# The same instructions of a two-layer hybrid decoder trunk, ordered on each engine by a timeline model of time

## The chip, the cores and the metric

One core of a Trainium2 chip. The time is that of the whole program on the device, in microseconds (us); the runs shown are single executions, and their median is the kernel's time. A profile is one more execution, recorded by the hardware profiler, and its span goes from the first to the last instruction.

## What is computed

A sequence of 256 tokens of width 1024 goes through two layers, everything in fp32. Cut to what matters:

```python
for i in range(DEPTH):                      # DEPTH = 2
    h = h + 0.5 * swiglu(rmsnorm(h), ...)   # first feed-forward half step
    u = rmsnorm(h)
    (q, c_kv, q_idx, w_idx, k_idx, x_pool, z, xbc, dt_raw, gate_raw) = split(u @ w_in[i])
    y_attn = dsa_attention(...)             # indexer picks 64 keys, 8 heads
    y_pool = pool_mixer(x_pool, ...)        # windows of 2, 4, 8, 16
    y_ssd  = ssd_mixer(z, xbc, dt_raw, ...) # causal conv, chunked scan, gate, norm
    merged = (g_attn * (y_attn @ w_br_attn[i]) + g_pool * (y_pool @ w_br_pool[i])
              + g_ssd * (y_ssd @ w_br_ssd[i]))
    h = h + merged @ w_out[i]
    h = h + 0.5 * swiglu(rmsnorm(h), ...)   # second half step
    h = h + sigmoid(rmsnorm(h) @ w_g[i]) * (p[i] @ w_p[i])   # per-layer embedding
return rmsnorm(h)
```

## The kernel before

The weights are streamed once, in units of 128 x 1024 fp32 (512 KB). `load` (L128 to L130) does three things for each unit: SP fetches it as `raw`, ACT casts it to a high part `whi` (L129), and DVE takes the residue `wlo` = `raw` - `whi` (L130). A product is then three matmuls, L152 (high by high), L153 (low activation by high weight) and L154 (high activation by low weight, the one that needs `wlo`), each of 128 x 128 weights by 256 columns; a unit gives 24 of them. There are four buffers each of `raw`, `whi` and `wlo`, and `unit` asks for a unit three ahead of its use. PSUM is used as four banks for the large products (tag "mm") and four for everything else ("aux"), both from `bank`.

Each layer goes through these stages:

- FFN1 (about 15 to 200 us in layer 1), then the norm before the mix. `rnorm` sums squares (L203, L206 on ACT, L208 on DVE), adds over partitions with a matmul by ones (L232), takes the reciprocal root on DVE (L181 to L195), makes two diagonal matrices (L239, L240) and spreads the factor over the partitions with two matmuls (L246), which ACT copies to `rs_r` (L248).
- The mix, 200 to 430 us: input projections, a first weave of columns, conv (L618, L620, L623), indexer (L656 to L679) and gates; then a second weave, in which the generators of the scan (`ssd`, L834 to L875), attention (L640, L701 to L726), the pools and the gates take turns (`weave`, L609). L712 are transposes; L845 is the scan's matmul into 64 columns, L640 the attention's matmul from 64 rows.
- The lift: eight steps of 48 matmuls. A step fills one bank p1 (attention and pools, 24 matmuls) and half a bank p2 (scan, 24 matmuls). L587 reads p1 and frees it; L592 reads p2 and frees it, but L591 before it multiplies by `rs_r`, the factor of the scan's norm, so that no p2 is freed before that `rs_r` is there. L593 and L594 add up, L168 and L169 split the result for the output product (L312 and on).
- FFN2 and the per-layer embedding, then the second layer alike, and a final norm.

What sets the order: each engine runs its own list in order. The program is written in one sequence, and the tile scheduler makes the engines' lists from it, by the instructions' dependences, buffers and priorities; the kernel steers it with the order of its generators and with `issue_after`. Line 1113 in `program`, which builds everything twice (the second time with the order of the weight units that the first has noted), opens the context that does this.

In the rows and orders below, a name like `wlo_3022` is one buffer's content, numbered in the order of the program; the profile leaves these numbers out.

Of the kernel before, what the change touches and what calls it, by code (L numbers as in the profile page):

```python
# [1103 lines left out]
def program(arrays):  # L1104

    order = None
    for last in (False, True):
        nc = bacc.Bacc("TRN2", target_bir_lowering=False, num_devices=1,
                       dynamic_dma_scratch_size=1024)
        ins = {k: nc.dram_tensor(f"in_{k}_dram", v.shape, F, kind="ExternalInput").ap()  # L1110
               for k, v in arrays.items()}
        out = nc.dram_tensor("out_0_dram", (2, P, D), F, kind="ExternalOutput").ap()
        with tile.TileContext(nc) as tc, ExitStack() as ctx:
            b = Builder(ctx, tc, ins, out, order)
            b.build()
        order = b.used
    return nc
# [8 lines left out]
```

## Time and profile before

| | us |
|---|---|
| median of 3 runs (lowest to highest) | 1342.96 (1341.96 to 1343.63) |
| the profiled execution's own time | 1343.21 |
| its span | 1341.4 |
| busy in the span: PE | 1319.0 (98%) |
| busy: DVE | 1047.8 (78%) |
| busy: ACT | 744.4 (55%) |
| granted TensorE clock, mean | 0.998 |

The program has 28355 instructions. Busy time of PE is the union of its matmuls as the profile draws them; their ends are modelled. Weight fetches move 248 MB in the span, a mean of 185 GB/s.

### The profile page before, as it was taken

The page shows a single profiled execution, that of the slowest core. Times are in us where ns is not written, and L with a number is a line of the kernel's source. Part 1 is how long each engine was busy: PE and PEld are TensorE (multiplying, and loading weights), DVE is VectorE, ACT ScalarE, POOL GpSimd, SP SyncE. Part 2 cuts the span into 40 slices and gives each one's busy share as a digit, 9 for nine tenths or more (in the row PEclk, how much of TensorE's full clock was granted, in tenths as well). Part 3 has the DMA queues.
Part 4 walks back from the last instruction along what each step waited for, and adds up shares of the span by engine and source line. Part 5 has one row for each costly group of instructions (what it writes and reads, how often), then busy time and mean ns, then how long its engine had stood idle before and what let it go on. Part 6 is the DMA issues. An engine that isn't in the chain of part 4 may idle for free.

```text
span 1341.4 us, 28355 instructions
## 1 busy us (share of the span) xinstructions
PE 1319.0 (98%) x11502; PEld 1299.4 (97%) x11502; DVE 1047.8 (78%) x1967; ACT 744.4 (55%) x1209; POOL 3.4 (0%) x17
## 2 busy tenths in 40 slices
PE   8999999999999999999999999999999999999997
PEld 7999999999899999999999999999998999999997
DVE  7777668987989787766887776789789887777666
ACT  5554446557754555544654554556577545555454
POOL 0000000000000000000000000000000000000000
PEclk9999999999999999999999999999999999999999
DMA  7666656566456666666656666646654666666661
GB/s 257 191 194 197 192 160 197 158 196 187 146 178 188 193 203 190 193 198 192 188 180 199 191 195 193 186 148 189 203 165 135 198 196 197 197 190 197 193 193 62
DMA packets 72386, 248.25 MB, mean 185 GB/s; under 512 B 7936, under 2 KB 10304, under 8 KB 72256
## 3 DMA queue, kind: packets, MB, share of 16 engines
q1 hardware_dynamic: 71392, 245.17, 59.3%
q8 instruction: 90, 1.47, 0.5%
q10 hardware_dynamic: 864, 1.28, 0.3%
q14 instruction: 40, 0.33, 0.1%
HBM read 245.33 MB, written 1.08 MB: 184 GB/s over the span
## 4 chain that ended last, share of the span: by engine, by line
PE 88%; DVE 8%; ACT 2%; issue 1%; DMA 0%; SPq 0%; DVEq 0%; ACTq 0%
PE mm L152 27%; PE mm L153 27%; PE mm L154 27%; DVE wlo L130 3%; ACT whi L129 1%; PE aux L640 1%; DVE t L620 1%; PE aux L726 1%; PE aux L845 1%; PE aux L152 1%; PE aux L153 1%; PE aux L154 1%; DVE rs_t L193 0%; DMA raw<-in_w_dram 0%; PE aux L712 0%
## 5 line engine op out<-in xcount | busy, mean ns | idle before, releaser
L129 ACT CAST whi<-raw 128x1024 fp32r<-128x1024 f32 (+1 forms) x457 | 475.8, 1045 | 484.9 <-issue 245.1
L152 PE MATMUL mm<-uh,whi 128*128 128x256 f32 x2560 | 712.9, 279 | 7.4 <-ACT whi L146 6.3
L154 PE MATMUL mm<-uh,wlo 128*128 128x256 f32 x2560 | 710.4, 278 | 2.8 <-DVE wlo L130 2.6
L153 PE MATMUL mm<-ul,whi 128*128 128x256 f32 x2560 | 711.5, 278 | 0.1
L130 DVE TENSOR_TENSOR wlo<-raw,whi 128x1024 fp32r<-128x1024 f32 (+1 forms) x457 | 554.2, 1215 | 200.8 <-ACT whi L129 198.1
L152 PEld LDWEIGHTS mm<-uh,whi 128*128 128x128 f32 x2560 | 482.0, 188 | 10.5 <-ACT whi L146 6.3
L154 PEld LDWEIGHTS mm<-uh,wlo 128*128 128x128 f32 x2560 | 482.2, 188 | 4.8 <-DVE wlo L130 3.7
L153 PEld LDWEIGHTS mm<-ul,whi 128*128 128x128 f32 x2560 | 482.2, 188 | 3.0 <-issue 2.1
L154 PE MATMUL mm<-gh,wlo 128*128 128x256 f32 x704 | 194.3, 276 | 0.0
L152 PE MATMUL mm<-gh,whi 128*128 128x256 f32 x704 | 194.3, 276 | 0.0
L153 PE MATMUL mm<-gl,whi 128*128 128x256 f32 x704 | 194.3, 276 | 0.0
L154 PEld LDWEIGHTS mm<-gh,wlo 128*128 128x128 f32 x704 | 132.1, 188 | 0.0
L153 PEld LDWEIGHTS mm<-gl,whi 128*128 128x128 f32 x704 | 132.1, 188 | 0.0
L152 PEld LDWEIGHTS mm<-gh,whi 128*128 128x128 f32 x704 | 132.1, 188 | 0.0
L152 PE MATMUL mm<-a,whi 128*128 128x256 f32 x256 | 70.9, 277 | 0.0
L153 PE MATMUL mm<-a,whi 128*128 128x256 f32 x256 | 70.7, 276 | 0.0
L154 PE MATMUL mm<-a,wlo 128*128 128x256 f32 x256 | 70.7, 276 | 0.0
L152 PEld LDWEIGHTS mm<-a,whi 128*128 128x128 f32 x256 | 48.1, 188 | 0.0
L153 PEld LDWEIGHTS mm<-a,whi 128*128 128x128 f32 x256 | 48.1, 188 | 0.0
L154 PEld LDWEIGHTS mm<-a,wlo 128*128 128x128 f32 x256 | 48.1, 188 | 0.0
L345 DVE TENSOR_TENSOR t<-mm,rs_r 128x256 f32<-128x256 f32 x88 | 37.3, 423 | 10.1
L172 ACT ACTIVATE uh<-h,cc 128x256 fp32r<-128x256 f32 x64 | 31.8, 504 | 18.5 <-DVE h L317 13.7
(213 smaller groups left out, 1114.4 us busy)
## 6 DMA issues: line engine op xcount, KB each, us to landing
raw<-in_w_dram SPq DMA_DIRECT2D x447, 512.0 KB, 3.9
ab<-rates SPq DMA_DIRECT2D x16, 256.0 KB, 3.7
raw<-in_w_dram SPq DMA_DIRECT2D x8, 352.0 KB, 3.2
raw<-in_w_dram SPq DMA_DIRECT2D x4, 256.0 KB, 3.4
ab<-rates SPq DMA_DIRECT2D x8, 128.0 KB, 4.1
h<-in_x_dram SPq DMA_DIRECT2D x2, 256.0 KB, 4.2
h<-in_x_dram SPq DMA_DIRECT2D x1, 512.0 KB, 6.3
t<-in_p_dram ACTq DMA_DIRECT2D x2, 256.0 KB, 4.8
```

Source lines behind the costliest of these rows:

```text
L129: nc.scalar.copy(hi[:, :n], raw[:, :n])
L130: nc.vector.tensor_tensor(lo[:, :n], raw[:, :n], hi[:, :n].bitcast(F), op=OP.subtract)
L152: mm(ps, a[0], b[0], start=start, stop=False)
L153: mm(ps, a[0], b[1], start=False, stop=False)
L154: mm(ps, a[1], b[0], start=False, stop=stop)
L172: self.nc.scalar.mul(hi, src, scale)
L345: nc.vector.tensor_tensor(t, p1[0], r, op=OP.mult)
L620: nc.vector.scalar_tensor_tensor(c[:, k:], ps[:, :S - k], w[:, 3 - k:4 - k], c[:, k:], op0=OP.mult, op1=OP.add)
L640: self.nc.tensor.matmul(ps[:, j * nk:(j + 1) * nk], q[x][rows, c, qs], key(y, c)[rows, :nk], start=(x + y == 0), stop=(y == 1))
L726: nc.tensor.matmul(py[o:o + 64, hd // 2 * P:(hd // 2 + 1) * P], vt[:, b, hd * 64:(hd + 1) * 64], x[:, j * nb + b], start=(b == 0), stop=(b ...
L845: nc.tensor.matmul(ps[b:b + 64, k * P:(k + 1) * P], xt[:, h, h0 + j], m[:, j], start=True, stop=True)
```

## The change

```diff
-        with tile.TileContext(nc) as tc, ExitStack() as ctx:
+        with tile.TileContext(nc, schedule_with_timeline_sim=True) as tc, ExitStack() as ctx:
```

The scheduler now picks, engine by engine, what is ready first by its own model of how long each instruction takes. The instructions, their shapes, the DMAs and the buffers stay the same; only the order on the engines is another: 2067 lines of difference on PE, 1655 on DVE, about 1000 on ACT, on SP only some fetches of the scan's rates that come after one to four weight fetches more, none on POOL. The moves sit in the first 20 us, at the end of FFN1, in the whole mix, in the lift's first steps, and around the norms' L246 later; both layers are changed alike.

Place one, the first weave on DVE (about 234 to 241 us). `wlo_3022` and `wlo_3058` are the residues of two weight units, t_443 and t_448 the indexer's scores, idxw its top-k work, t_440 and t_452 the conv's. Before:

```order
L661 TENSOR_SCALAR gl_2499<-t_443_3013,sm_2500 128x128
L663 SCALAR_TENSOR_TENSOR gl_2499<-t_443_3013,sm_2500,gl_2499 128x128 x3
L663 SCALAR_TENSOR_TENSOR gl_2499<-t_448_3050,sm_2500,gl_2499 128x128 x4
L674 MAX m_454_3108<-gl_2499 128x8
L130 TENSOR_TENSOR wlo_3022<-raw_3020,whi_3021 128x1024
L675 MATCH_REPLACE idxw_3107<-m_454_3108,gl_2499 128x128
L674 MAX m_454_3108<-idxw_3107 128x8
```

and now:

```order
L663 SCALAR_TENSOR_TENSOR gl_2499<-t_443_3013,sm_2500,gl_2499 128x128 x2
L130 TENSOR_TENSOR wlo_3022<-raw_3020,whi_3021 128x1024
L663 SCALAR_TENSOR_TENSOR gl_2499<-t_448_3050,sm_2500,gl_2499 128x128
L620 SCALAR_TENSOR_TENSOR t_440_2981<-mm_2891,cc_93,t_440_2981 128x255
L663 SCALAR_TENSOR_TENSOR gl_2499<-t_448_3050,sm_2500,gl_2499 128x128
L620 SCALAR_TENSOR_TENSOR t_440_2981<-mm_2891,cc_93,t_440_2981 128x254
L663 SCALAR_TENSOR_TENSOR gl_2499<-t_448_3050,sm_2500,gl_2499 128x128
L130 TENSOR_TENSOR wlo_3058<-raw_3056,whi_3057 128x1024
```

The residue `wlo_3022` stood behind all seven L663 and the first L674; now it stands ahead of the last four L663 and of every L674, and so do the residues after it.

Place two, the second weave on PE (about 319 to 325 us). `aux_4242` are transposes of attention weights, `aux_4207` the scan's matmuls into 64 columns, `mm_4294` a product of the gates. Before, 20 rows lay between the two kinds:

```order
L154 MATMUL mm_3961<-uh_2725,wlo_3982 128x256
L712 MATMUL aux_4242<-ident,t_599_4155 128x128 x4
L152 MATMUL mm_4085<-uh_2725,whi_4057 128x256
...
L153 MATMUL mm_4294<-ul_2726,whi_4087 128x256
L845 MATMUL aux_4207<-t_609_4208,ul_4037 64x128 x4
L154 MATMUL mm_4294<-uh_2725,wlo_4088 128x256
```

and now:

```order
L154 MATMUL mm_4294<-uh_2725,wlo_4088 128x256
L712 MATMUL aux_4242<-ident,t_599_4155 128x128
L845 MATMUL aux_4207<-t_609_4208,ul_4037 64x128
L712 MATMUL aux_4242<-ident,t_599_4155 128x128
L845 MATMUL aux_4207<-t_609_4208,ul_4037 64x128
L712 MATMUL aux_4242<-ident,t_599_4155 128x128
L845 MATMUL aux_4207<-t_609_4208,ul_4037 64x128
L712 MATMUL aux_4242<-ident,t_599_4155 128x128
L845 MATMUL aux_4207<-t_609_4208,ul_4037 64x128
L152 MATMUL mm_4294<-uh_2725,whi_4087 128x256
```

Both groups come later, and one group of four L845 has become four groups of one. Over the whole program there are 26 such groups of L845 where there were 18, and 20 of L640 where there were 12.

Place three, the lift's start on DVE (about 404 us). `mm_5329`, `mm_5471` are p1 of its second and fourth step; `mm_5231`, `mm_5330`, `mm_5401`, `mm_5472` are p2 of steps one to four. Before:

```order
L240 SCALAR_TENSOR_TENSOR t_787_5281<-ident,rs_y_5040,t_786_5280 128x128 x2
L587 SCALAR_TENSOR_TENSOR t_802_5391<-gh_2498,mm_5329 128x512
L130 TENSOR_TENSOR wlo_5363<-raw_5361,whi_5362 128x1024
L591 SCALAR_TENSOR_TENSOR t_793_5322<-gl_2499,rs_r_5038 128x256
L591 SCALAR_TENSOR_TENSOR t_803_5393<-gl_2499,rs_r_5038 128x256
L592 TENSOR_TENSOR t_793_5322<-t_793_5322,mm_5231 128x256
L592 TENSOR_TENSOR t_803_5393<-t_803_5393,mm_5330 128x256
```

and now:

```order
L240 SCALAR_TENSOR_TENSOR t_787_5281<-ident,rs_y_5040,t_786_5280 128x128 x2
L587 SCALAR_TENSOR_TENSOR t_822_5533<-gh_2498,mm_5471 128x512
L130 TENSOR_TENSOR wlo_5505<-raw_5503,whi_5504 128x1024
L593 TENSOR_TENSOR t_822_5533<-t_822_5533 128x256
L591 SCALAR_TENSOR_TENSOR t_793_5322<-gl_2499,rs_r_5038 128x256
...
L591 SCALAR_TENSOR_TENSOR t_843_5677<-gl_2499,rs_r_5038 128x256
L592 TENSOR_TENSOR t_793_5322<-t_793_5322,mm_5231 128x256
L592 TENSOR_TENSOR t_803_5393<-t_803_5393,mm_5330 128x256
L592 TENSOR_TENSOR t_813_5464<-t_813_5464,mm_5401 128x256
L592 TENSOR_TENSOR t_823_5535<-t_823_5535,mm_5472 128x256
```

The norm's steps and what hangs on them stand two lift steps later: six L591 come in a row, and the first L592, which frees the first p2, stands after the L587 of the fourth step and not of the second.

## Rows read from the trace of the kernel before

**Rows 1.** The page: busy time, share of the span, instructions.

```profile
PE 1319.0 (98%) x11502; PEld 1299.4 (97%) x11502; DVE 1047.8 (78%) x1967; ACT 744.4 (55%) x1209; POOL 3.4 (0%) x17
```

**Rows 2.** Timeline of PE in FFN1: start us, length us, instruction, [idle before <-releaser].

```profile
100.02 0.28 PE L154 MATMUL mm<-uh,wlo 128*128 128x256 f32 x1
100.14 0.28 PE L152 MATMUL mm<-uh,whi 128*128 128x256 f32 x1
```

**Rows 3.** Stretches: from:to and length, busy us by engine, PEclk, DMA share, GB/s.

```profile
322.00:342.00 20.00, 19.68 (x182) 17.61 (x181) 18.28 (x42) 16.35 (x40) 0.00 (x0) 1.00 0.54 170
342.00:375.00 33.00, 32.08 (x275) 28.29 (x274) 31.75 (x73) 24.30 (x52) 0.00 (x0) 1.00 0.49 148
...
400.00:420.00 20.00, 19.84 (x175) 19.65 (x174) 19.50 (x47) 8.84 (x12) 0.00 (x0) 1.00 0.59 177
420.00:660.00 240.00, 239.71 (x2115) 239.54 (x2114) 179.07 (x296) 124.28 (x183) 0.00 (x0) 1.00 0.63 194
```

**Rows 4.** PE's waits, first weave (200:262, 860:922): us in total, times, longest.

```profile
PE mm L154 <- DVE wlo L130: 1.8, 2, 1.0
...
PE mm L154 <- DVE wlo L130: 0.8, 1, 0.8
```

**Rows 5.** Timeline of DVE, first weave.

```profile
234.91 2.75 DVE L663 SCALAR_TENSOR_TENSOR gl<-t,sm,gl 128x128 f32<-128x128 f32 x7
238.12 0.29 DVE L674 MAX8 m<-gl 128x8 f32<-128x128 f32 x1 [0.46 <-POOL gl L667]
238.33 1.21 DVE L130 TENSOR_TENSOR wlo<-raw,whi 128x1024 fp32r<-128x1024 f32 x1
```

**Rows 6.** PE's waits in the second weave of layer 1 (322:380).

```profile
PE aux L712 <- ACT t L707: 0.5, 1, 0.5
PE aux L845 <- DVE t L840: 0.5, 2, 0.3
```

**Rows 7.** Timeline of PE around L246, in the lift and at FFN2's end.

```profile
404.25 0.38 PE L246 MATMUL aux<-t,onesr 128*128 128x256 f32 x1 [0.15 <-DVE t L239]
...
650.58 0.28 PE L154 MATMUL mm<-uh,wlo 128*128 128x256 f32 x1
651.15 0.35 PE L246 MATMUL aux<-t,onesr 128*128 128x256 f32 x1 [0.29 <-DVE t L239]
```

**Rows 8.** Timeline of PE at two groups of L845 (second weave).

```profile
325.61 0.39 PE L154 MATMUL mm<-uh,wlo 128*128 128x256 f32 x1
325.83 0.28 PE L152 MATMUL mm<-uh,whi 128*128 128x256 f32 x1
...
335.74 0.28 PE L152 MATMUL mm<-uh,whi 128*128 128x256 f32 x1
335.94 0.66 PE L845 MATMUL aux<-t,ul 128*64 128x128 f32 x8
```

**Rows 9.** DVE and ACT by line, 375:424: count, busy us, mean ns, idle before.

```profile
L130 DVE TENSOR_TENSOR wlo<-raw,whi 128x1024 fp32r<-128x1024 f32 x18 | 21.8, 1222 | 3.7 <-ACT whi L129 3.5
L587 DVE SCALAR_TENSOR_TENSOR t<-gh,mm 128x512 f32<-128x512 f32 x5 | 3.4, 683 | 0.5 <-PE mm L154 0.5
L591 DVE SCALAR_TENSOR_TENSOR t<-gl,rs_r 128x256 f32<-128x256 f32 x8 | 3.3, 419 | 0.0
L208 DVE TENSOR_TENSOR acc<-acc,t 128x256 f32<-128x256 f32 x4 | 1.7, 420 | 0.0
...
L248 ACT COPY rs_r<-aux 128x256 f32<-128x256 f32 x1 | 0.4, 373 | 0.1
```

**Rows 10.** The start: timeline of ACT, and L206 by count: duration ns min/median/max.

```profile
4.80 0.51 ACT L172 ACTIVATE uh<-h,cc 128x256 fp32r<-128x256 f32 x1 [2.06 <-DMA cc<-in_cc_dram]
...
L206 ACT ACTIVATE t<-h x7: 400/402/412, 8.1 to 13.5; 128x256 f32<-128x256 f32 x7
...
10.64 1.03 ACT L129 CAST whi<-raw 128x1024 fp32r<-128x1024 f32 x1
```

**Rows 11.** Timeline of PE at the low part of u, before the first weave.

```profile
215.31 0.51 PE L152 MATMUL mm<-uh,whi 128*128 128x256 f32 x2 [0.33 <-ACT uh L168]
```

## The prediction

> **What bounds the kernel now.** I read the page first: PE is busy for 1319.0 of 1341.4 us, DVE for 78% and ACT for 55% [rows 1]. In steady work a 256-column matmul starts 0.12 us after the one before [rows 2]; the drawn length of 0.28 overlaps the next. No order makes these starts closer, so a change of order can only remove PE's idle time, 1341.4 - 1319.0 = 22.4 us, or add to it. Then I read the stretches for where that idle time lies. The FFNs have nearly none: 0.3 us in 240 [rows 3]. The second weave has 0.32 in its first 20 us and 0.92 in the next 33, with DVE busy 18.28 and 31.75 there; in the lift DVE is busy for 19.50 of 20 us while PE loses only 0.16 [rows 3]. The granted clock is 1.00 in all four stretches, the 2.4 GHz level. So two bounds are close to each other in the mix: PE sets the end, and DVE is 92 to 98% full. Last I read what ends PE's waits, which gives the terms below. A wait's cost is its listed length plus 0.17, since the list counts from the drawn end of the matmul before, and that lies 0.28 - 0.11 = 0.17 after the next possible start.
>
> About 0.2%, 2.7 us, is what a measurement of this kernel can tell from no change: faster is below 1340.3, slower above 1345.6.
>
> **What goes.** First weave: PE waited twice for a residue in layer 1, 1.8 us in all, and once in layer 2, 0.8 [rows 4]; with 0.17 each that is 2.1 + 1.0 = 3.1 us. The cause is seen on DVE: seven L663 take 2.75 us, then L674 waits 0.46 for POOL, and only then comes the residue, done at 239.54 [rows 5]. In the new order this residue stands ahead of four L663 and the L674, so it is 4 x 0.39 + 0.46 + 0.2 = 2.2 us earlier, more than the 1.0 it was late. The residues after it have the top-k work behind them too. I take all **3.1** off; the least would be 1.0, if ACT's casts were the next to be late.
>
> Second weave: the idle time in the two stretches is 0.32 + 0.92 = 1.24 us, over some six waits, of which two kinds carry a name: L712 for attention's exponentials and L845 for L840 [rows 6]. With 6 x 0.17 that is 2.2 a layer. In the new order these L712 and L845 stand 30 to 180 rows later on PE, at 0.11 us a row 3 to 20 us, with gate products put ahead of them, while their producers on DVE move less. What is late next would be the scan's tail, which moves into the lift; that is priced below. I take nine tenths of 2 x 2.2, so **4.0**; the least is 2.
>
> Norms: in FFN2's end L246 starts 0.57 us after the matmul before, 0.46 too late [rows 7], once a layer; it moves 35 to 45 rows later, 4 to 5 us, and the wait goes: 0.9. The lift's L246 loses 0.15 + 0.17 = 0.32 [rows 7], twice 0.6. Together **1.5**. Gains: 3.1 + 4.0 + 1.5 = 8.6.
>
> **What comes.** Lift: the steps of the scan's norm come two lift steps later, and p2 banks are freed only once `rs_r` is there. There are four banks, and by then three p2 hold one each. The fourth step's p1 fills the last; its p2 must wait for L587 to free it, 0.68 us [rows 9], against two L246 that fill 0.2 of that: 0.5. The fifth step's p1 needs the first L592. Counted from the end of the fourth p1 on DVE: L587 0.68, a residue 1.22, L593 0.42, six L591 at 0.42, one L592 0.42 [rows 9], together 5.3. PE has in that time the 0.7 until L587 is through and 24 matmuls at 0.113, 2.7, so 3.4: a gap of 1.9. I take 1.5 of it, since short instructions in a row overlap at their ends: eight L591 were busy for 3.3 us and stood among others. 0.5 + 1.5 is 2.0, and I add 0.5 for L232, which now waits for the last L208 with DVE full. **5.0** for two layers; bounds 0 (banks turn out free earlier) and 10.
>
> Groups: 8 more groups of L845 and 8 more of L640. A matmul of 64 rows or columns starts 0.20 us after a full one, and the second full one after a group 0.22 after the first, not 0.11 [rows 8]: 0.09 + 0.11 = 0.20 a group, and 16 x 0.20 is **3.2**. The bounds are 1.5 (where a group falls into a wait) and 5.4. The Trainium skill, "TensorEngine Tiling (Array Packing)", Key Properties, says that a change of tiling mode drains TensorE, which speaks against this change. If a drain meant that the next start stands behind the drawn end of the last matmul, each way would cost 0.17 and the term would be 5.4; the row shows 0.09 and 0.11, so I go by the row.
>
> Start: ACT now does all eight squares before the second unit's cast, of which four were done before. 4 x 0.40 [rows 10] is 1.6 us later for that cast, and the one square placed ahead of the first L172 falls partly into ACT's wait of 2.06 for the DMA. The residue after the cast has some 0.3 to 1 us of room. **1.0**, bounds 0 and 2.
>
> Low part of u: the wait of 0.33 + 0.17 = 0.5 at L152 [rows 11] goes, but the norm's L246 before it stand 15 and 40 rows later, so the factor comes about 4 us later and the first L153 that needs the low part waits in its place, by my count 0.8 to 1.3. **1.0** for two layers net, bounds -0.5 and 2. The moved fetches on SP are of rates used many units later; transfers are three units ahead, so I cost them at nothing. If that cover were gone, one unit's transfer would show, a few us.
>
> **Sum.** -8.6 + 5.0 + 3.2 + 1.0 + 1.0 = +1.6. At the tail nothing of size moves. On the profiled execution's 1343.21 this is 1344.8; the median of the runs shown lies 0.25 lower, so **1344.5 us**, which can't be told from no change.
>
> **Rivals.** *Faster, 1338.5.* The lift's waits are hidden, because PSUM banks or splits that DVE has made ahead cover them; DVE had 0.5 us to spare at L587 there [rows 9]. Then 5.0 becomes 1.0 and the groups fall partly into what idle time is left, 2.0 for 3.2: 1344.5 - 5.2 = 1339.3, and with a start at 0.2 it is 1338.5. For it: most waits of before are of a kind that order cures, and a timeline model knows the banks. Against it: `rs_r` demonstrably stands behind six more instructions and a residue.
>
> *Slower, 1348.7.* DVE's backlog decides. The scan's tail (two instructions of L587's size, 0.68, and twelve of L208's, 0.42 [rows 9]) is 6.4 us, and in the new order much of it stands within the lift's first steps. A lift step asks DVE for two residues, one L587 and five of 0.42, 2.44 + 0.68 + 2.1 = 5.2 of PE's 48 x 0.113 = 5.4 us, so eight steps work off 1.8 us of backlog. If all of the tail falls in, 6.4 - 1.8 = 4.6 a layer is lost in place of 2.5: +4.2, 1348.7. It decides from the point where the tail left over at the lift's start exceeds about 4 us: the splits' lead of one to three units (2.7 us each) covers the first part.
>
> *Drained groups, 1346.7*: every added group costs 0.34, as worked out above: +2.2.
>
> *Nothing moves in effect*: PE 98% busy, and what waits is only passed from one place to another; that is my forecast's own neighbourhood, 1343.
>
> **Chances.** Forecast and its neighbourhood 0.45; faster rival 0.25; backlog 0.23; drained groups 0.07. The last two are the slower side: 0.30. The range goes from the faster rival's 1338.5, less half a us, to the backlog's 1348.7 and 2.3 more, a start at its bound of 2 and what of the gains might stay: 1338 to 1351. Outside lie a lift that costs 10, and gains that all hold with no cost at all, together under 0.2.
>
> **What the profile after should show.** No wait of L154 for L130 near 240, 259 and 919. In the second weave PE idle below 0.3 us a stretch, but more starts 0.2 apart at L845 and L640. In the lift two gaps on PE, one of about 0.5 and one of 1 to 2 us, ended by L587 and L592 of DVE, and DVE busy over 95%. L152 at the start later by some tenths. I am wrong if the lift shows no gap at its fourth and fifth step, if the second weave keeps its waits, or if residues in the lift are late by several us.

## The result: slower by 0.7%, and the profile after

| | before | after |
|---|---|---|
| median, 4 runs each (lowest to highest), us | 1342.88 (1341.96 to 1343.63) | 1352.14 (1351.26 to 1354.44) |
| ratio of the medians, 95% interval | | 1.007 (1.0058 to 1.0083) |
| profiled execution: own time, span, us | 1343.21, 1341.4 | 1351.39, 1349.3 |

The change made the kernel 9.3 us slower in the median and 7.9 us in the profiled span. That is outside the range of the prediction and beyond the slower rival. The page of after, to be set against [rows 1] (busy time, share, instructions):

```profile
span 1349.3 us, 28295 instructions
...
PE 1323.1 (98%) x11502; PEld 1300.3 (96%) x11502; DVE 1040.5 (77%) x1967; ACT 741.4 (55%) x1209; POOL 5.1 (0%) x17
```

Each engine has the same number of working instructions as before; the 60 that the program has fewer (28355 before) are none of those counted on the page. PE's busy time grew by 4.1 us, its idle time by 26.2 - 22.4 = 3.8: matmuls are not only later here and there, some are also drawn longer. To find the places I subtracted, for one and the same count n, the start of the n-th matmul in before from its start in after. Both programs have 11502, so the difference is the time lost or won up to there. Where the orders differ it swings by some tenths, so the stages are cut at places where both programs have done the same work; the lift begins just before its L246 in before. It is worked out from the two traces' matmul records:

| stretch of the program (layer 1, layer 2) | won (-) or lost (+), us | forecast for it |
|---|---|---|
| start and FFN1 of layer 1 | 0.0 | +1.0 |
| FFN1's end and first weave | -1.06, +0.89 | -3.1 + 1.0 |
| second weave | -0.49, -0.97 | -4.0 + 3.2 |
| lift, with its norm's L246 | +1.87, +1.81 | +5.0 - 0.6 |
| FFN2's first product | +0.74, +0.73 | 0 |
| embedding, up to its last columns | -0.43, -0.16 | -0.9 |
| norm between the layers, with FFN1's start | +4.91 | 0 |
| sum | +7.84 | +1.6 |

The last row but one holds more than half of the loss, and the prediction had no term for it. What ends PE's waits there (after, 660:700; line, waited for, us in total, times, longest):

```profile
PE mm L152 <- DVE t L345: 1.2, 1, 1.2
PE aux L246 <- DVE t L239: 0.6, 1, 0.6
PE mm L152 <- ACT uh L172: 0.4, 1, 0.4
```

The third wait stands in before as well. L345 is the first feed-forward step that multiplies by `rs_r`, the norm's factor. Here is how late its chain has become, first on DVE in before:

```profile
677.04 0.42 DVE L208 TENSOR_TENSOR acc<-acc,t 128x256 f32<-128x256 f32 x1
...
678.29 0.16 DVE L234 TENSOR_SCALAR rs_v<-aux 128x2 f32<-128x2 f32 x1 [0.83 <-PE aux L232]
...
684.19 0.61 DVE L240 SCALAR_TENSOR_TENSOR t<-ident,rs_y,t 128x128 fp32r<-128x128 f32 x2
...
688.27 0.42 DVE L345 TENSOR_TENSOR t<-mm,rs_r 128x256 f32<-128x256 f32 x1
```

and in after:

```profile
680.29 0.42 DVE L208 TENSOR_TENSOR acc<-acc,t 128x256 f32<-128x256 f32 x1
...
681.93 2.36 DVE L130 TENSOR_TENSOR wlo<-raw,whi 128x1024 fp32r<-128x1024 f32 x2 [1.23 <-ACT whi L129]
684.21 0.15 DVE L234 TENSOR_SCALAR rs_v<-aux 128x2 f32<-128x2 f32 x1
...
690.47 0.61 DVE L240 SCALAR_TENSOR_TENSOR t<-ident,rs_y,t 128x128 fp32r<-128x128 f32 x2
691.08 1.23 DVE L130 TENSOR_TENSOR wlo<-raw,whi 128x1024 fp32r<-128x1024 f32 x1
692.22 0.42 DVE L345 TENSOR_TENSOR t<-mm,rs_r 128x256 f32<-128x256 f32 x1
```

The last square sum L208 is 3.25 us later. L234 is 5.92 later, for two reasons. PE's L232, which adds that sum over the partitions, now stands 35 matmuls further on (no. 5826 in place of 5791), first in before and then in after:

```profile
677.75 0.50 PE L232 MATMUL aux<-ones,acc 128*128 128x1 f32 x4
...
682.96 0.50 PE L232 MATMUL aux<-ones,acc 128*128 128x1 f32 x4
```

And two residues stand in front of L234 on DVE. So the diagonal factors L240 come 6.28 us later. PE's next L152 wants the bank that L345 frees, and has nothing ahead of it by then. PE's timeline in after, with two waits in a row (0.63 and 1.17):

```profile
690.71 0.81 PE L246 MATMUL aux<-t,onesr 128*128 128x256 f32 x2 [0.63 <-DVE t L239]
692.69 0.39 PE L152 MATMUL mm<-uh,whi 128*128 128x256 f32 x1 [1.17 <-DVE t L345]
...
693.99 0.41 PE L154 MATMUL mm<-uh,wlo 128*128 128x256 f32 x1
694.21 0.41 PE L152 MATMUL mm<-uh,whi 128*128 128x256 f32 x1
```

The last two starts are 0.22 us apart, not 0.11 as in [rows 2]. The stretches of after show why (columns as in [rows 3]; the last but two is the granted clock):

```profile
688.00:692.00 4.00, 2.81 (x21) 2.25 (x19) 3.68 (x10) 1.74 (x3) 0.00 (x0) 1.00 0.93 311
692.00:696.00 4.00, 3.31 (x18) 3.31 (x19) 3.23 (x9) 1.17 (x3) 0.00 (x0) 0.68 0.62 208
696.00:700.00 4.00, 4.00 (x33) 4.00 (x33) 1.75 (x4) 1.67 (x3) 0.00 (x0) 0.90 0.00 1
```

After the pause the granted clock was 0.68 over four microseconds, so part of them ran at the 1.2 GHz level, and some 16 matmuls started 0.213 us apart. That is a part of the growth of busy time: 16 x 0.10 = 1.6 us. The 4.91 us of this norm are 0.6 lost ahead of L246, 2.7 at L246 and L345, and these 1.6.

At the other places the waits are short and named. In the lift (after, 385:425), the gaps that were forecast:

```profile
PE mm L152 <- DVE t L592: 1.2, 1, 1.2
PE mm L152 <- DVE t L587: 0.4, 1, 0.4
```

At FFN1's end (after, 200:220) the wait of [rows 11] has gone and two others stand there:

```profile
PE mm L152 <- ACT whi L129: 1.1, 1, 1.1
PE mm L153 <- DVE ul L169: 0.4, 1, 0.4
```

At FFN2's first product (after, 470:485), where before had none:

```profile
PE mm L152 <- DVE t L345: 0.5, 1, 0.5
```

Here it is L246 itself that stands later: its second matmul is no. 4048 in place of 4028, and L345 on DVE waits for the `rs_r` that is made from it (after):

```profile
479.28 0.42 DVE L345 TENSOR_TENSOR t<-mm,rs_r 128x256 f32<-128x256 f32 x1 [0.72 <-ACT rs_r L248]
```

The waits of [rows 4] and [rows 6] have no counterpart. Against [rows 3], the second weave of after:

```profile
322.00:342.00 20.00, 20.00 (x169) 17.81 (x167) 16.43 (x34) 14.90 (x34) 0.00 (x0) 1.00 0.59 191
342.00:375.00 33.00, 33.00 (x295) 30.48 (x293) 28.87 (x68) 24.79 (x53) 0.00 (x0) 1.00 0.55 166
...
400.00:420.00 20.00, 18.41 (x158) 17.89 (x157) 18.93 (x44) 7.64 (x8) 0.00 (x0) 1.00 0.59 189
```

PE has no idle time left in the weave, and 1.59 us of it in the lift.

### The profile page after: what moved, and what is told of

Same layout as the page of the kernel before. It is cut to its first block, busy times and chain, and to the rows that moved or that the text cites. A ratio compares the mean times of both kernels' runs of the same rounds, so it can differ in the third digit from the quotient of the medians.

```text
span 1349.3 us, 28295 instructions
## 1 busy us (share of the span) xinstructions
PE 1323.1 (98%) x11502; PEld 1300.3 (96%) x11502; DVE 1040.5 (77%) x1967; ACT 741.4 (55%) x1209; POOL 5.1 (0%) x17
## 4 chain that ended last, share of the span: by engine, by line
PE 94%; DVE 3%; ACT 1%; issue 1%; DMA 0%; DVEq 0%; ACTq 0%
PE mm L152 29%; PE mm L154 29%; PE mm L153 29%; PE aux L640 1%; PE aux L845 1%; DVE wlo L130 1%; PE aux L152 1%; PE aux L153 1%; PE aux L154 1%; ACT whi L129 1%; PE aux L726 1%; PE aux L712 1%; DVE t L439 0%; DMA h<-in_x_dram 0%; DVE t L591 0%
## 5 line engine op out<-in xcount | busy, mean ns | idle before, releaser
L129 ACT CAST whi<-raw 128x1024 fp32r<-128x1024 f32 (+1 forms) x457 | 475.8, 1045 | 502.0 <-issue 249.5
L152 PE MATMUL mm<-uh,whi 128*128 128x256 f32 x2560 | 709.0, 279 | 12.2 <-ACT whi L146 6.9
L152 PEld LDWEIGHTS mm<-uh,whi 128*128 128x128 f32 x2560 | 480.4, 188 | 16.3 <-ACT whi L146 6.9
L152 PE MATMUL mm<-gh,whi 128*128 128x256 f32 x704 | 193.7, 276 | 0.0
L152 PEld LDWEIGHTS mm<-gh,whi 128*128 128x128 f32 x704 | 131.9, 188 | 0.0
L152 PE MATMUL mm<-a,whi 128*128 128x256 f32 x256 | 70.0, 277 | 3.2 <-DVE t L592 2.4
L152 PEld LDWEIGHTS mm<-a,whi 128*128 128x128 f32 x256 | 47.6, 188 | 3.8 <-ACT whi L129 2.7
L345 DVE TENSOR_TENSOR t<-mm,rs_r 128x256 f32<-128x256 f32 x88 | 37.2, 423 | 11.1 <-ACT rs_r L248 1.4
L350 DVE SCALAR_TENSOR_TENSOR t<-t,t 128x256 f32<-128x256 f32 x88 | 37.4, 425 | 3.1
```

The source lines that it names most:

```text
L129: nc.scalar.copy(hi[:, :n], raw[:, :n])
L152: mm(ps, a[0], b[0], start=start, stop=False)
L345: nc.vector.tensor_tensor(t, p1[0], r, op=OP.mult)
L350: nc.vector.scalar_tensor_tensor(g, th, 1.0, t, op0=OP.add, op1=OP.mult)
```

## The experiments

**The device.** The program is built a third time. In that build `pin` ties the instructions of chosen stages, on chosen engines, to each other in the order that the default scheduler gave them; these ties are marked as needing no synchronisation, and the working instructions stay the same. All the rest is left to the model. The stages are F1 (FFN1), M (from FFN1's end to the first weave), W1 (first weave), m (between the weaves), W2 (second weave), L (lift and output product), F2 (FFN2), P (embedding) and end. Each kernel differs in `STAGES` and `ENGINES` alone, unless a diff says more; the pair's first number is the layer, from 0.

```diff
+STAGES = {(0, 'P'), (1, 'F1')}
+ENGINES = {'PE', 'Pool', 'Activation', 'SP', 'DVE'}
...
+    for name, engine in ref:
+        if name not in by or stage[name] not in STAGES or engine not in ENGINES:
+            continue
+        if engine in last:
+            tc.add_manual_dep(by[name], last[engine], ...
+        last[engine] = name
...
-    for last in (False, True):
+    for n in range(3):
...
-        with tile.TileContext(nc, schedule_with_timeline_sim=True) as tc, ExitStack() as ctx:
+        with tile.TileContext(nc, schedule_with_timeline_sim=n == 2) as tc, ExitStack() as ctx:
```

**e1_bound: the default order around the norm between the layers.** The diff is the one above.

> The new order, but with the instructions of layer 1's embedding stage and layer 2's FFN1 chained on every engine in the order of before. Theory A (the loss is a sum of local waits, and the largest is the norm between the layers: 4.5 of the 7.9 us of span, from DVE taking L234 behind residues, and with it a fall of the granted clock): 1352.1 - 4.5 = about 1347.5, no PE gap at 690 us, granted clock 1.00 there. Theory B (the loss is a lower clock or a slower pace over the whole program, and the gap at 690 is only where it shows): above 1350, with another stretch below 1.00.

Measured: 1347.37 us (1345.45 to 1349.14, 6 runs), a ratio of 1.0035 (1.0023 to 1.0047) to before, 4.8 us under after's median. From the matmul before the embedding's last columns to FFN1 in steady work it loses nothing (3.07 us behind before, then 3.03), where after lost 4.91, and the clock holds:

```profile
690.00:694.00 4.00, 4.00 (x38) 4.00 (x36) 3.33 (x6) 2.51 (x6) 0.00 (x0) 1.00 0.77 235
```

So about half of the loss is the order of the stages around this one norm, 1.6 us of lower clock included.

**e2_bound_dve: the same stages, on DVE alone.**

```diff
-ENGINES = {'PE', 'Pool', 'Activation', 'SP', 'DVE'}
+ENGINES = {'DVE'}
```

> As e1, but only DVE is chained; PE, ACT and SP stay with the model's order there. Theory A1 (DVE's order is the cause: two residues stand before L234, and each waits for a cast on ACT): most of e1's gain, about 1348. Theory A2 (ACT is the cause: its casts come late behind the uh of the last columns, and DVE only shows it): less than half of e1's gain, above 1350.

Measured: 1353.53 us (1352.40 to 1356.22), ratio 1.0084 (1.0069 to 1.0099). Above 1350, as in theory A2, but the stretch is worse than in either order, which neither theory had; the whole time can't be told from after's (1.0058 to 1.0083). On DVE, in its own order again:

```profile
686.90 0.16 DVE L234 TENSOR_SCALAR rs_v<-aux 128x2 f32<-128x2 f32 x1 [4.39 <-PE aux L232]
```

DVE stands 4.39 us, because PE's L232 stayed late; in those microseconds DVE does nothing else. The stretch costs 9.5 us in place of 4.9. DVE's order alone does not heal the chain; all engines' orders together do (e1_bound). PE's alone was not run.

**e3_lift: the default order in the lift, both layers, all engines** (`STAGES = {(0, 'L'), (1, 'L')}`).

> The new order, but with the lift's and output product's instructions chained in the order of before in both layers; the scan's tail, which belongs to the second weave, stays where the model put it. Theory A (the lift loses 2.35 us a layer because rs_r comes two steps later and p2 banks are held): 1352.1 - 4.7 = about 1347.4, no gaps ended by L587 and L592. Rival (the scan's tail on DVE is the backlog, whatever order the lift has): PE waits for L232 or L246 instead, above 1350.

Measured: 1363.04 us (1361.38 to 1363.11), ratio 1.0148 (1.0131 to 1.0165). The theory that the lift's own order alone was at fault fell; its rival holds. PE now waits for the last square sum of the scan, which the model has left late in the second weave's tail:

```profile
400.52 0.98 PE L232 MATMUL aux<-ones,acc 128*128 128x1 f32 x4 [4.16 <-DVE acc L208]
```

That square sum stood on DVE in before at

```profile
386.35 0.42 DVE L208 TENSOR_TENSOR acc<-acc,t 128x256 f32<-128x256 f32 x1
```

and stands in after 17 us later:

```profile
403.38 0.42 DVE L208 TENSOR_TENSOR acc<-acc,t 128x256 f32<-128x256 f32 x1
```

Given this tail, the model's lift, which moves the norm back by two steps, is the better one: 1.9 us lost a layer against 7.2 in layer 1 here. Of the 7.2, some 2.9 are 29 matmuls 0.213 us apart behind the long wait, with a granted clock of 0.55 and 0.60 in 400:404 and 404:408. So what the lift loses depends on the tail that the second weave hands to it. The second weave alone was not put back in any run.

**e4_mix_only: the model's order up to the lift's start, the default one after it** (`STAGES`: L, F2, P, end of both layers and F1 of the second).

> The model's order is kept in the start and in the mix up to the lift; lift, output product, FFN2, embedding stage and layer 2's FFN1 are chained as before. Theory A: what is left is the front of the mix (-1.1 and +0.5 us in the two layers) and the second weave (-1.0 and -1.1), so 1342.9 - 2.7 = about 1340.2. Theory B (waits taken away in the weaves come back wherever DVE is full): 1342.9 or above.

Measured: 1356.99 us (1354.82 to 1359.11), ratio 1.0107 (1.0092 to 1.0122). It was to be faster than before, and is not, for the reason seen in e3_lift: PE waits 4.2 us at L232 for the last L208, in either layer. Behind the lift, in FFN2 by the default order, nothing is lost (7.69 us behind before at the lift's end and behind FFN2's first product), where after lost 0.74.

**e5_first_weave_only: the model's order in the first weave and up to the second, the default one everywhere else** (`STAGES` holds all but W1 and m).

> The order of before in all stages but the first weave and the few instructions around it, which keep the model's order. Theory A: only the gains of the first weave stay. In the changed kernel's trace the matmuls from number 1800 to 2600 came 1.9 us closer, those from 7500 to 8400 0.8 us, so 1342.6 - 2.7 = about 1339.9, with no PE wait for a residue near 240, 260 and 919 us. Rival (the first weave's gain is only the low part of u being late before it, taken back): 1342.6.

Measured: **1339.93 us** (1339.42 to 1341.13, 11 runs) against 1342.91 (17 runs of before), ratio 0.9979 (0.9970 to 0.9987). Faster than both kernels. PE has no wait between 215 and 262 us, and the stretch wins 2.2 us in layer 1 and 1.0 in layer 2. These 3.2 us are the forecast's first gain, alone; the start, too, is in the order of before here.

**e6_weave2_and_lift_back: the default order in second weave and lift** (`STAGES`: W2 and L, both layers).

> The new order, but the second weave and the lift with the output product are chained as before in both layers. Theory A (the second weave saves about 1 us a layer on PE by putting off the scan, and the lift pays 2.35 for the late tail): net 1.4 + 0.8 = 2.2 less, 1352.1 - 2.2 = about 1349.9, no gap ended by L587 or L592, and the waits of before at L712 and L845 back. Rival (the tail is late for a reason before the second weave): the gaps in the lift stay or L232 waits 4 us as in e3, 1352 or more.

Measured: 1348.47 us (1347.74 to 1349.58), ratio 1.0042 (1.0028 to 1.0055), 3.7 under after. The two stretches together stand level with before (-0.33 us ahead and behind them), where after loses 1.4 and 0.8; the gaps at L587 and L592 are gone, and the old waits of [rows 6] are back:

```profile
PE aux L845 <- DVE t L840: 0.5, 2, 0.3
PE aux L712 <- ACT t L707: 0.5, 1, 0.5
PE aux L246 <- DVE t L239: 0.2, 1, 0.2
```

What the model wins in the second weave it pays back, and more, in the lift. FFN2, left to the model here, still loses 0.74 in layer 1 (from 0.33 ahead to 0.41 behind), so that loss does not come from the lift.

**e7_u_split_back: the default order at FFN1's end** (`STAGES`: M, both layers).

> The new order, but the stage between FFN1 and the first weave (the norm's L246, the split of u, the first projections) is chained as before in both layers. Theory A: the two gaps of 1.24 and 0.71 us at the low part of u go and the 0.5 of before comes back: about 1.2 a layer, 1352.1 - 2.4 = about 1349.7. Rival (the gaps come from DVE having too much to do there, in any order): the wait moves to a residue in the first weave, 1352.

Measured: 1347.92 us (1346.30 to 1349.31), ratio 1.0035 (1.0023 to 1.0047). No wait is left between 200 and 262 us, and the stretch of FFN1's end and first weave is 1.4 us shorter than after's in either layer, 2.8 together. The time fell by 4.2; in the profiled execution, 1.6 of it is the lower clock of after between the layers, which did not come here (see e9_fill_the_gap).

**e8_pe_free_in_weave2: as e5, but PE's order in the second weave left to the model**, with the other engines' kept.

```diff
+    (0, 'W2'): ('DVE', 'Activation', 'SP', 'Pool'),
+    (1, 'W2'): ('DVE', 'Activation', 'SP', 'Pool'),
```

> As e5 (first weave by the model, everything else as before), but in the second weave only DVE, ACT, POOL and SP are chained as before; PE's order there is the model's. Theory A (PE's waits in the second weave can be filled with gate products, and what cost the lift was DVE's part of the scan, which now keeps its place): the waits of 2.2 us a layer mostly go, 1339.9 - 3.5 = about 1336.5. Rival (the scan's matmuls, 15 to 56 rows later on PE, make DVE wait and the scan's tail late again): L232 or L246 waits in the lift, 1341 or more.

Measured: 1353.93 us (1353.11 to 1354.47), ratio 1.0084 (1.0069 to 1.0099). The time is in the rival's range, the waits are not the rival's: in the lift PE waits 0.2 for L246, as before, and not at all for L232. Between 320 and 400 us PE now asks for things before the others have made them:

```profile
PE mm L154 <- DVE wlo L130: 4.0, 5, 1.9
PE mm L152 <- ACT whi L129: 1.5, 1, 1.5
PE aux L712 <- ACT t L707: 1.4, 1, 1.4
```

The second weave loses 6.8 us in layer 1 where the model's whole order wins 0.5.

**e10_pe_free: PE free in all stages but M, the other engines free in W1 and m alone.**

> As e8, but PE's order is the model's in FFN1 of both layers, lift, output product, FFN2 and embedding stage too; DVE, ACT, POOL and SP are chained as before, save in the first weave, and the stage before it is chained on PE as well. Theory A (the loss came from DVE and ACT putting the norm's chain late; with them fixed, PE's free order only fills waits): at or below e8. Theory B (the model is too early or too late with the norm's matmuls on PE: L232 of the lift stands 70 rows earlier, L246 28 rows later than before): PE waits at L232 by some us a layer, above 1345.

Measured: 1358.51 us (1357.93 to 1359.52), ratio 1.0120 (1.0105 to 1.0135). That is in theory B's range, but again PE does not wait at L232 in the lift. The waits of e8 for residues and casts are there (2.9 and 1.5 us in 320:440), and 4.8 us more are lost at the norm between the layers, with waits of PE in 660:705 as

```profile
PE mm L152 <- ACT uh L172: 1.6, 1, 1.6
PE mm L152 <- DVE t L345: 1.4, 1, 1.4
```

**e9_fill_the_gap: after's order, with 13 matmuls put into the pause at 690 us**, seven before the two L246 and six behind them. Nothing reads what they write.

```diff
+            for _ in range(fill[0]):
+                self.dummy.append(nc.tensor.matmul(pr[:, :S], self.onesr, x, start=True, stop=True).ins)
...
             nc.scalar.copy(r, pr[:, :S])
+            for _ in range(fill[1]):
+                self.dummy.append(nc.tensor.matmul(pr[:, :S], self.onesr, x, start=True, stop=True).ins)
```

> The changed kernel's own order, with 13 matmuls added whose result is overwritten or not read: seven ahead of the two L246 of layer 2's FFN1 norm and six behind their copy, where PE stood idle. The output stays the same. Theory A (of the 4.9 us there some 1.7 is the lower clock, 17 matmuls 0.213 apart in place of 0.113, and it falls because PE stands idle before): the granted clock stays 1.00 between 690 and 700, about 1.7 us less in that stretch. Rival (the low clock has another cause than the idle time): the same 17 matmuls at 0.213, and the added ones cost up to 1 us.

Measured: 1351.67 us (1349.84 to 1353.04), ratio 1.0064 (1.0048 to 1.0081); the medians don't tell it from after. In the stretch itself the clock held:

```profile
694.00:698.00 4.00, 4.00 (x37) 4.00 (x37) 2.71 (x7) 2.16 (x5) 0.00 (x0) 1.00 0.51 152
```

and it cost 1.81 + 13 x 0.113 = 3.3 us in place of 4.9. But this does not show that the filling held the clock. e7 and e6 have the same three waits unfilled (1.2, 0.6, 0.4), and their clock held as well; here is e7:

```profile
688.00:692.00 4.00, 2.12 (x14) 1.56 (x14) 3.41 (x11) 1.83 (x3) 0.00 (x0) 1.00 0.81 271
692.00:696.00 4.00, 4.00 (x38) 4.00 (x37) 3.08 (x7) 2.42 (x5) 0.00 (x0) 1.00 0.37 118
```

There the stretch cost 3.3 us too (from -1.02 to 2.28). And e9, which has after's waits at FFN1's end (1.1 and 0.4), shows the clock falling at that place, where after's stayed at 1.00:

```profile
212.00:216.00 4.00, 3.57 (x21) 3.57 (x22) 4.00 (x11) 0.62 (x1) 0.00 (x0) 0.70 0.51 135
```

It cost e9 1.6 us more than after lost there (2.45 against 0.82). In layer 2 the same waits, 1.1 and 0.4, stand in after, e6 and e9: the clock stayed at 1.00 in after and fell to 0.76 in e6 (876:880). So the waits are shown to cost 3.3 us at the norm between the layers; a further 1.6 comes or doesn't come in one execution or another, with the same order and the same waits. What decides it stays open.

**e11_first_weave_and_later_spread: as e5, and on PE the L246 of the lift and of the embedding's norm six matmuls later.**

```diff
+        if x[0] in spreads and stage[x[0]][1] in ("L", "P"):
+            held.append([x, LATER])
```

> As e5, and on PE alone the L246 of the lift and of the embedding stage's norm stand five to six matmuls later, in both layers (0.6 to 0.7 us). Theory A: the waits of 0.32 and 0.45 us at L246 go, since DVE needs rs_r only 1 us later: 2 x 0.77 = 1.5 less, 1339.9 - 1.5 = about 1338.4. Rival (whoever needs rs_r is late by the same time, as in the changed kernel's FFN2): no gain, 1339.9, with waits for L592 or for the banks of the embedding stage.

Measured: **1337.70 us** (1337.49 to 1339.27, 5 runs) against 1342.48, ratio 0.9964 (0.9950 to 0.9977): the fastest of all. None of the L246 that were moved waits any more (one at 201 us, of the norm before the mix, was not moved and waits 0.4); in the lift (compare [rows 7]):

```profile
401.62 0.28 PE L246 MATMUL aux<-t,onesr 128*128 128x256 f32 x1
```

Six matmuls, 0.7 us, are enough to hide a wait of 0.15 to 0.3. The gains are 0.5 us at each of the four places. The model had moved them 35 to 45 in the embedding's norm and 93 to 96 in the lift.

## Why the prediction was wrong, step by step

**The step that failed is "Norms": it counted two norms and put the others at nothing.** The prediction said of the embedding's L246 that "it moves 35 to 45 rows later, 4 to 5 us, and the wait goes: 0.9", and took 0.6 for the lift's. These gains came: PE wins 0.5 us at each of the four places, 2.1 in all for the 1.5 taken. But the change moves steps of the norms ahead of the FFNs as well, and for these the sum has no term and no reason why there is none. They cost 4.9 us between the layers and 0.7 in each FFN2, +6.4 in all, as large as the whole miss, 7.8 - 1.6 = 6.2 us in the profiled executions (1352.1 - 1344.5 = 7.6 in the medians). Of the 6.4, 1.6 is the lower clock, which came in this execution and not in e6 and e7. The step asked which matmul waits for the norm and not who waits for the norm's result: L345 needs `rs_r` and frees the bank that PE wants next. Ahead of FFN2 it is L246's later place that makes `rs_r` late. Between the layers it is L232's, with the residues ahead of L234; L246 itself waits there. e1_bound shows the loss between the layers: with the default order in the two stages around it, nothing is lost. For FFN2, the loss is gone in e4, with the default order there, and stays in e6, which has the default order in the second weave and the lift ahead of it but not in FFN2. The lift was treated with the right question ("what hangs on it"), the norms were not.

**Low part of u: 1.0 taken, 3.0 measured**, outside its own bounds. This step did ask who waits, but looked at DVE's `ul` (0.4 + 0.17 = 0.6 measured, 0.8 to 1.3 forecast) and not at ACT. There the cast of the next unit stands behind the split:

```profile
209.31 1.63 ACT L168 CAST uh<-t 128x256 fp32r<-128x256 f32 x5
210.85 1.04 ACT L129 CAST whi<-raw 128x1024 fp32r<-128x1024 f32 x1
```

The late factor holds five of the casts L168 up into one row, the weight's L129 waits behind them, and PE's first L152 of the next unit waits 1.1 for that. e7_u_split_back puts 1.4 a layer on it, so 2.8 of the 3.0.

**First weave: -3.1 taken, -3.2 measured**, alone in e5. From start to start, the three waits for residues stood 2.1 and 1.0 us above the pace of 0.113 in before, and all three are gone in e5, as the prediction took it. Six of the eight new groups of L640 lie here too; the smaller gaps that went with the waits make up for them.

**Second weave with groups: -0.8 taken, -1.5 measured.** The waits went, but there were three a layer and not six: from start to start they cost 1.49 and 1.52 us above 0.113, so 3.0 went and not 4.0. What is left, 3.0 - 1.5 = 1.5, is the cost of the groups with all else that changed there, against the 3.2 taken for the whole program. Transposes with L845 between, in after:

```profile
324.48 0.33 PE L712 MATMUL aux<-ident,t 128*128 128x128 f32 x1
324.74 0.43 PE L845 MATMUL aux<-t,ul 128*64 128x128 f32 x2
325.10 0.33 PE L712 MATMUL aux<-ident,t 128*128 128x128 f32 x1
```

The two changes of shape are in these 0.62 us from L712 to L712. No run has the groups alone. (DVE's share in the first stretch of the weave is 18.28 of 20, so 91% and not the 92 of the prediction.)

**Lift: +4.4 taken, +3.7 measured.** Both gaps came where the prediction put them, ended by L587 (0.39 + 0.17 = 0.6, forecast 0.5) and by the first L592 (1.20 + 0.17 = 1.4, forecast 1.5); counted from start to start, PE falls back 2.4 us a layer there, and L246's wait gives 0.5 back. The 0.5 more for L232 did not come on PE, since the model has put L232 late too. That the scan's tail is late, the backlog rival's place (its last L208 ends 17 us later), was seen only with e3 and e4: there PE pays 4.2 us at L232 for it, which the delay costed at 2.5 avoids.

**Start: +1.0 taken, 0.0 in this pair of executions.** The 0.0 hides a cost: before's execution kept the slow pace of the last section until 14.7 us, after's until 10.8. Where the pace doubled at about the same time, the new order of the start is 0.6 to 0.7 us later at matmul no. 300 (e7 at 10.4 against e5, with the order of before, at 10.2: 0.16 and 0.76 ahead of before; e6 at 14.6 against before at 14.7: 0.71 behind). That is inside the bounds of the step.

Without the norms' three places the table adds up to 7.84 - 6.38 = +1.5 us, against +1.6 in the sum. That nearness is partly luck: u cost 2.0 more than taken, and the second weave, the lift and the start 0.7, 0.7 and 1.0 less. What broke the forecast were the norms ahead of the three FFNs.

## What to carry to other kernels

When a reordering moves a reduction or a norm, follow its result to everyone who waits for it, on every engine it crosses, and do so for every norm that moved, not only for those whose wait goes: four waits that went won 2.1 us here, and three norms that nobody had waited for cost 6.4. One engine's order from one schedule did not fit the others' orders from another: parts of two schedules on different engines (e2, e8, e10), or a stage behind another's tail (e3, e4), were no better than the worse of the two whole schedules, and in e3, e4 and e10 clearly worse. Test such a schedule stage by stage, keep the stage that wins (e5), and move single instructions by as little as their wait asks (e11).

## What the runs showed of the hardware that was not expected

**The clock falls at a pause in some executions and not in others.** With the same waits of 1.2, 0.6 and 0.4 us between the layers it fell in after (granted 0.68) and held in e6 and e7 (1.00); with waits of 1.1 and 0.4 at FFN1's end it held in after and fell in e9 (0.70), and in layer 2 it fell in e6 too (0.76). Each of these falls cost 1.6 us, some 16 matmuls 0.213 apart. The runs of after spread more than those of before, 3.2 us from lowest to highest against 1.7 (1.7 in e5 as well), and the slower ones have the lower mean clock: 0.996 and 0.996 at 1351.26 and 1351.39 us, 0.995 at 1352.88, 0.994 at 1354.44.

**The slow pace at the start ends at another time in each run.** The first matmuls of the program start 0.213 us apart, as at the 1.2 GHz level, though the profile's clock column reads 1.00 there. In executions with after's order at the start the pace doubled at 10.8 us (after), 18.3 (e1), 10.9 (e2), 11.2 (e3), 19.2 (e4), 14.6 (e6) and 10.4 (e7); with the order of before, at 14.7 (before) and 10.2 (e5). PE's timeline of e4 at that point:

```profile
19.03 0.32 PE L154 MATMUL mm<-uh,wlo 128*128 128x256 f32 x1
19.18 0.28 PE L152 MATMUL mm<-uh,whi 128*128 128x256 f32 x1
```

At matmul no. 300 e4 is 2.42 us behind before, e1 1.99, e7 0.16 and e3 0.26 ahead. The Trainium skill, "TensorE: Matmul & The Clock Gate", section "What's actually happening", says that the throttled state is the default and that activity releases it, at a point that shifts by about half a microsecond with the moment of the first matmul. The trace agrees in the direction, slow first and fast later. The size differs: here, where the first matmuls come with waits between them, 8.8 us lie between the earliest and the latest. By no. 300 that is 2.7 us, and the programs carry it to their ends. A difference at the start that one pair of executions shows is to be read only between executions whose pace doubled at the same time.
